# Sample attention of a decoder step: narrow products ordered by a priority of their own, the last-arriving input first, and the first head's key parts split off one step ahead

## The chip, the cores and the metric

The kernel runs on one core of one Trainium2 chip. The metric is the device time of one execution in microseconds. A core has five engines with queues of their own: TensorE (PE: matrix products; PEld is its weight load, which overlaps), VectorE (DVE), ScalarE (ACT), GpSimd (POOL) and SyncE (SP). Each engine takes the instructions of its queue strictly in order. An instruction whose input isn't there holds back everything behind it on that engine.

## The reference, cut to what matters

One layer of a hybrid decoder: a gated FFN, token mixing (differential attention beside an mLSTM), and a second gated FFN. It is computed for a prompt of 512 tokens, and for 8 samples with 4 new tokens each, whose attention looks back on 512 tokens in a paged cache. The change touches the attention: that of the samples, and the first block of that of the prompt.

```
past_k = cache_k[l][page_table].reshape(DB, -1, H_ATT, ATT_KDIM)
past_v = cache_v[l][page_table].reshape(DB, -1, H_ATT, ATT_DV)
...
logits = jnp.einsum('bqhcd,bkhcd->bchqk', q, k) * (ATT_DQ ** -0.5)
logits = jnp.where(mask, logits + bias, -jnp.inf)
p = jax.nn.softmax(logits, axis=-1)
a = p[:, 0] - lam * p[:, 1]
return jnp.einsum('bhqk,bkhd->bqhd', a, v)
```

All arrays are float32. There are 4 heads with keys of 2 x 64 and values of 128 columns, and 4 cache pages of 128 tokens for each sample.

## The kernel before, in words

**Wide products.** The activations lie transposed, channels on the partitions, in two halves of 288 and 256 tokens. Each weight tile of 128x128 is split into a high and a low part (L210 on ACT, L211 on DVE), and `mm3` issues three products for each tile: L224, L225, L226. A half of one output tile takes 8 tiles of 128 channels, so 24 such products of 288 or 256 columns stand in a row.

**Side work.** While the projections of the mixing stage run (`run(project(...))` in `mix`), every half of a projection is followed by one step of a set of generators: `attn_head` (queue "prep"), `attn_block` (queue "attn"), `attn_samples` (queue "smp"), and the mLSTM's. A step traces a few instructions, up to its `yield`. The order of the instructions on each engine is then made at compile time by a scheduler: of the instructions that it holds to be ready it takes the one of the highest priority, and the priority follows the order in which the program traced them. `high_priority(offset=...)` raises it for what is traced in its block; `issue_after(ins)` puts what its block traces on an engine behind `ins` there.

**Prompt attention.** `key_parts` splits a head's keys into high and low parts (L936 on ACT, L937 on DVE), `query_parts` does it for the 128 queries of a block (L946, L948; their tile `vb` exists once). The products of queries and keys are L964. In the kernel before, the first step of `attn_block` for block 0 of a head makes the parts, and its second step issues L964.

**Sample attention.** `attn_samples` works through two groups g of four samples j. Pages come by an indirect DMA that POOL issues (`page`, L1013) into the tile `pgin`, of which there are 7. Key pages are transposed (L1039), copied by ACT (L1040) to `pgT` (3 of it), and multiplied with the queries in *narrow* products: L1027 has only 32 columns of weights, one for each head, in four column strips of the array (`tile_position=(0, 32 * h)`). One call of `scores` makes 4 of them, and two calls come together. L1066 does the same for the new keys. After the softmax (L1069 to L1092), narrow products of 512 columns follow: four with the new values (L1098), and for each of the 4 value pages pg four with the cached values (L1102), one for each sample j. The four value pages for pg + 1 are requested after the four products of pg are traced. At that point three of the seven `pgin` tiles hold key pages ahead for g = 1, while g = 0 runs, and four hold the value pages in use. A narrow product of one strip can run beside those of the other three. In fp32 each of them is two instructions in the trace.

The queue of POOL holds, besides the page requests, the loads and stores of the mLSTM's states (L1212, L1279) and small copies (L1459).

Of the kernel before, what the change touches and what calls it, by code (L numbers as in the profile page):

```python
# [22 lines left out]
NS = NB * NT  # L23
# [6 lines left out]
NPG = PAST // PAGE  # L30
H = 4
# [22 lines left out]
AHEAD = 3  # L54
NBK = 32
# [123 lines left out]
class _Builder:  # L179
# [722 lines left out]
    def attn_head(self, h, k, v, side):  # L902
        nc = self.nc
        hd = self.hd
        kt = hd.tile([128, 4, 128], F32, name="kt")
        vt = hd.tile([128, 4, 132], F32, name="vt")
        for qb in range(4):
            side.add("attn", self.attn_block(h, qb, self.X[:, 4 + h, :], k, vt))
            if qb < 2:
                yield  # L910
# [40 lines left out]
    def attn_block(self, h, qb, q, k, vt):  # L951
        nc = self.nc
        wk = self.wk
        n = (qb + 1) * 128
        if qb == 0:
            self.key_parts(k)
            self.query_parts(q[:, 0:n])
            yield
# [35 lines left out]
        po = self.ps_tile()  # L994
# [11 lines left out]
    def attn_samples(self):  # L1006
# [14 lines left out]
        for g in range(2):  # L1021
# [3 lines left out]
            def scores(p, j, kT):  # L1025
                for h in range(H):
                    nc.tensor.matmul(lg[32 * h:32 * h + 32, p * 256:p * 256 + 256], lhsT=self.qz[:, 4 * g + j, h, :],  # L1027
                                     rhs=kT[:, h, :], start=j == 0, stop=j == 3, tile_position=(0, 32 * h))
            for p in range(NPG // 2):
                for j in range(4):  # L1030
# [10 lines left out]
                    if len(todo_scores) == 2:  # L1041
                        while todo_scores:
                            scores(*todo_scores.pop(0))
# [18 lines left out]
            while todo_scores:  # L1062
                scores(*todo_scores.pop(0))
            for j in range(4):
                for h in range(H):
                    nc.tensor.matmul(ln[32 * h:32 * h + 32, 0:NS], lhsT=self.qz[:, 4 * g + j, h, :], rhs=self.kas[:, h, :],  # L1066
                                     start=j == 0, stop=j == 3, tile_position=(0, 32 * h))
# [28 lines left out]
            for j in range(4):  # L1096
                sj = slice(32 * j, 32 * j + 32)
                nc.tensor.matmul(po[sj, :], lhsT=an[:, sj], rhs=vtok, start=True, stop=False, tile_position=(0, 32 * j))  # L1098
            for pg in range(NPG):
                for j in range(4):  # L1100
                    sj = slice(32 * j, 32 * j + 32)
                    nc.tensor.matmul(po[sj, :], lhsT=aT[:, pg * 128 + 32 * j:pg * 128 + 32 * j + 32], rhs=vps[j],  # L1102
                                     start=False, stop=pg == NPG - 1, tile_position=(0, 32 * j))
# [544 lines left out]
```

## Time and profile before

| what | value |
|---|---|
| time, median of 3 runs | 1174.2 us (1172.94 to 1174.42) |
| time of the profiled execution | 1173.48 us |
| span of the profiled execution | 1171.7 us |
| PE, PEld busy | 1156.8 us, 1119.6 us |
| DVE, ACT, POOL busy | 655.0 us, 524.5 us, 114.4 us |
| mean granted TensorE clock | 0.996 |

The span runs from the first instruction to the last, and the execution's own time has 1.8 us around it. In this kernel TensorE is busy nearly always, so the useful views are those that show where it is not: the stretches (busy time and granted clock in windows), what it waited for, and the order of time. Matmuls are pipelined, so the start of one to the start of the next tells what it costs; the duration of a single one in the profile is longer.

### The profile page before, as it was taken

To read this page: it belongs to the slowest core of one execution; us is meant where nothing else is said; L and a number is where in the kernel's file an instruction comes from. 1 tells how busy PE (TensorE), PEld (TensorE's weight loads), DVE (VectorE), ACT (ScalarE), POOL (GpSimd) and SP (SyncE) were. 2 spreads that over 40 slices of the span, in tenths; PEclk is the share of its full clock that TensorE was granted. 3 is DMA by queue.
4 is the path that set the end of the run, shared out by engine and by line. 5 is a ranking of instruction groups with operands and counts; after the bars stand their busy time and mean duration, and the time that the engine had idled before them with its cause. 6 is when DMAs were issued, how large, how long until landed. Compare 5 with 4: busy or idle time off the path is not lost. (4 is left out here: it accounts for less than half of the span.)

```text
span 1171.7 us, 22966 instructions
## 1 busy us (share of the span) xinstructions
PE 1156.8 (99%) x9202; PEld 1119.6 (96%) x9202; DVE 655.0 (56%) x1633; ACT 524.5 (45%) x1259; POOL 114.4 (10%) x155
## 2 busy tenths in 40 slices
PE   8999999999999999999999999999999999999997
PEld 8999999999999999899789879999999999999997
DVE  6655454544223698668676567885555454522334
ACT  6533332333323565667555566763333332332333
POOL 0000000000000043421234441000000000000000
PEclk9999999999999999999999999999999999999999
DMA  7322322232333464543355644532322323133333
GB/s 190 127 73 76 105 91 90 73 98 75 100 95 104 137 178 142 174 133 86 98 158 165 197 148 156 168 106 75 109 73 74 108 85 97 50 100 99 100 100 126
DMA packets 157545, 132.89 MB, mean 113 GB/s; under 512 B 5437, under 2 KB 149157, under 8 KB 157440
## 3 DMA queue, kind: packets, MB, share of 16 engines
q1 hardware_dynamic: 146576, 102.00, 29.8%
q0 software_dynamic: 8624, 27.05, 7.3%
q10 hardware_dynamic: 2240, 2.38, 0.7%
q8 instruction: 72, 1.18, 0.4%
q14 instruction: 33, 0.27, 0.1%
HBM read 122.35 MB, written 9.59 MB: 113 GB/s over the span
## 5 line engine op out<-in xcount | busy, mean ns | idle before, releaser
L224 PE MATMUL acc<-h,wh 128*128 128x256 f32 (+1 forms) x1896 | 552.6, 292 | 0.0
L225 PE MATMUL acc<-h,wh 128*128 128x256 f32 (+1 forms) x1896 | 547.6, 289 | 0.0
L226 PE MATMUL acc<-h,wl 128*128 128x256 f32 (+1 forms) x1896 | 545.0, 287 | 0.0
L211 DVE TENSOR_TENSOR wl<-raw,wh 128x512 fp32r<-128x512 f32 x378 | 251.2, 675 | 206.4 <-ACT wh L210 203.1
L224 PEld LDWEIGHTS acc<-h,wh 128*128 128x128 f32 x1896 | 357.0, 188 | 8.2 <-issue 7.5
L226 PEld LDWEIGHTS acc<-h,wl 128*128 128x128 f32 x1896 | 358.0, 189 | 0.7 <-issue 0.6
L225 PEld LDWEIGHTS acc<-h,wh 128*128 128x128 f32 x1896 | 357.3, 188 | 0.9 <-issue 0.4
L210 ACT CAST wh<-raw 128x512 fp32r<-128x512 f32 x378 | 225.6, 607 | 254.1 <-PE acc L225 208.9
L225 PE MATMUL acc<-ul,wh 128*128 128x288 f32 (+1 forms) x704 | 202.6, 288 | 0.0
L224 PE MATMUL acc<-uh,wh 128*128 128x288 f32 (+1 forms) x704 | 202.3, 287 | 0.0
L226 PE MATMUL acc<-uh,wl 128*128 128x288 f32 (+1 forms) x704 | 201.8, 287 | 0.0
L224 PEld LDWEIGHTS acc<-uh,wh 128*128 128x128 f32 x704 | 132.2, 188 | 0.1
L225 PEld LDWEIGHTS acc<-ul,wh 128*128 128x128 f32 x704 | 132.2, 188 | 0.1
L226 PEld LDWEIGHTS acc<-uh,wl 128*128 128x128 f32 x704 | 132.2, 188 | 0.1
L413 ACT CAST uh<-uu 128x288 fp32r<-128x288 f32 x88 | 36.9, 419 | 148.1 <-DVE uu L412 148.1
L411 DVE TENSOR_TENSOR uu<-acc,r 128x288 f32<-128x288 f32 (+1 forms) x84 | 37.0, 440 | 112.1 <-PE acc L226 106.8
L404 ACT ACTIVATE sg<-sg 128x288 f32<-128x288 f32 (+1 forms) x84 | 35.9, 430 | 93.6 <-DVE sg L396 93.6
L396 DVE TENSOR_TENSOR sg<-acc,r 128x288 f32<-128x288 f32 x84 | 37.0, 441 | 56.9 <-PE acc L226 52.4
L414 DVE TENSOR_TENSOR ul<-uu,uh 128x288 fp32r<-128x288 f32 x88 | 38.6, 439 | 22.1 <-ACT uh L413 22.0
L412 DVE TENSOR_TENSOR uu<-uu,sg 128x288 f32<-128x288 f32 x88 | 38.8, 441 | 7.1 <-ACT sg L404 1.6
L1335 POOL DMA_DIRECT2D x_keep<-X x2 | 1.8, 896 | 359.8 <-DVE X L327 359.8
L1013 POOL DMA_INDIRECT pgin<-in_cache_v_dram,idx x32 | 33.2, 1037 | 34.9 <-PE smp L1039 15.3
(388 smaller groups left out, 1088.2 us busy)
## 6 DMA issues: line engine op xcount, KB each, us to landing
raw<-in_ffn_w_gate_dram SPq DMA_DIRECT2D x20, 1024.0 KB, 5.3
raw<-in_ffn_w_up_dram SPq DMA_DIRECT2D x20, 1024.0 KB, 5.3
raw<-in_ffn_w_down_dram SPq DMA_DIRECT2D x20, 1024.0 KB, 6.1
raw<-in_w_in_dram SPq DMA_DIRECT2D x28, 512.0 KB, 4.6
raw<-in_ffn_w_down_dram SPq DMA_DIRECT2D x20, 384.0 KB, 3.6
raw<-in_w_out_dram SPq DMA_DIRECT2D x7, 1024.0 KB, 5.9
raw<-in_ffn_w_gate_dram SPq DMA_DIRECT2D x4, 512.0 KB, 5.9
raw<-in_ffn_w_up_dram SPq DMA_DIRECT2D x4, 512.0 KB, 6.9
```

What stands on the lines that cost most here:

```text
L210: nc.scalar.copy(out=wh[:, 0:n], in_=s)
L211: nc.vector.tensor_tensor(out=wl[:, 0:n], in0=s, in1=wh[:, 0:n].bitcast(F32), op=ALU.subtract)
L224: nc.tensor.matmul(ps, lhsT=wh, rhs=xh(k0 + k), start=st, stop=False)
L225: nc.tensor.matmul(ps, lhsT=wh, rhs=xl(k0 + k), start=False, stop=False)
L226: self.last_mm = nc.tensor.matmul(ps, lhsT=wl, rhs=xh(k0 + k), start=False, stop=sp).ins
L396: nc.vector.tensor_tensor(out=sg, in0=pg, in1=self.rs(hs, half), op=ALU.mult)
L404: nc.scalar.activation(out=sg, in_=sg, func=AF.Silu)
L411: nc.vector.tensor_tensor(out=uu, in0=pu, in1=self.rs(hs, half), op=ALU.mult)
L412: nc.vector.tensor_tensor(out=uu, in0=uu, in1=sg, op=ALU.mult)
L413: nc.scalar.copy(out=uh[:, m, sl], in_=uu)
L414: nc.vector.tensor_tensor(out=ul[m][:, sl], in0=uu, in1=uh[:, m, sl].bitcast(F32), op=ALU.subtract)
L1013: nc.gpsimd.indirect_dma_start(out=t[:, 0:512], out_offset=None, in_=caches[which], in_offset=IndirectOffsetOnAxis(ap=self.idx[:, b * NPG ...
```

## The change

Three edits, in `attn_samples`, `attn_head` and `attn_block`.

First, the narrow products get a priority far above their place in the program (`AHEAD_OF`), each group of 8 or 4 in a block of its own. Second, their order is turned: the newest key tile first in `scores`, the newest head first in the products with the new keys, the last-requested page first with the values. The products with the new keys come before the last scores (`issue_after`). Third, `attn_head` makes the key and query parts of head 0 itself, yields, and only then adds the blocks; block 0 of head 0 then yields without making them.

```diff
+AHEAD_OF = 20000
...
         kt = hd.tile([128, 4, 128], F32, name="kt")
         vt = hd.tile([128, 4, 132], F32, name="vt")
+        if h == 0:
+            self.key_parts(k)
+            self.query_parts(self.X[:, 4, 0:128])
+            yield
         for qb in range(4):
...
         if qb == 0:
-            self.key_parts(k)
-            self.query_parts(q[:, 0:n])
+            if h:
+                self.key_parts(k)
+                self.query_parts(q[:, 0:n])
             yield
...
-            def scores(p, j, kT):
-                for h in range(H):
-                    nc.tensor.matmul(lg[32 * h:32 * h + 32, p * 256:p * 256 + 256], lhsT=self.qz[:, 4 * g + j, h, :],
-                                     rhs=kT[:, h, :], start=j == 0, stop=j == 3, tile_position=(0, 32 * h))
+            def scores(todo):
+
+                with self.tc.high_priority(offset=AHEAD_OF):
+                    for p, j, kT in reversed(todo):
+                        for h in range(H):
+                            nc.tensor.matmul(lg[32 * h:32 * h + 32, p * 256:p * 256 + 256],
+                                             lhsT=self.qz[:, 4 * g + j, h, :], rhs=kT[:, h, :],
+                                             start=j == 1, stop=j == 2, tile_position=(0, 32 * h))
+                todo.clear()
...
                     if len(todo_scores) == 2:
-                        while todo_scores:
-                            scores(*todo_scores.pop(0))
+                        scores(todo_scores)
...
-            while todo_scores:
-                scores(*todo_scores.pop(0))
-            for j in range(4):
-                for h in range(H):
-                    nc.tensor.matmul(ln[32 * h:32 * h + 32, 0:NS], lhsT=self.qz[:, 4 * g + j, h, :], rhs=self.kas[:, h, :],
-                                     start=j == 0, stop=j == 3, tile_position=(0, 32 * h))
+            with self.tc.high_priority(offset=AHEAD_OF):
+                for j in range(4):
+                    for h in reversed(range(H)):
+                        mm = nc.tensor.matmul(ln[32 * h:32 * h + 32, 0:NS], lhsT=self.qz[:, 4 * g + j, h, :],
+                                              rhs=self.kas[:, h, :], start=j == 0, stop=j == 3, tile_position=(0, 32 * h))
+            with self.tc.issue_after(mm.ins):
+                scores(todo_scores)
...
             po = self.smp.tile([128, 512], F32, name="smp")
-            for j in range(4):
-                sj = slice(32 * j, 32 * j + 32)
-                nc.tensor.matmul(po[sj, :], lhsT=an[:, sj], rhs=vtok, start=True, stop=False, tile_position=(0, 32 * j))
-            for pg in range(NPG):
+            with self.tc.high_priority(offset=AHEAD_OF):
                 for j in range(4):
                     sj = slice(32 * j, 32 * j + 32)
-                    nc.tensor.matmul(po[sj, :], lhsT=aT[:, pg * 128 + 32 * j:pg * 128 + 32 * j + 32], rhs=vps[j],
-                                     start=False, stop=pg == NPG - 1, tile_position=(0, 32 * j))
+                    nc.tensor.matmul(po[sj, :], lhsT=an[:, sj], rhs=vtok, start=True, stop=False, tile_position=(0, 32 * j))
+            for pg in range(NPG):
+                with self.tc.high_priority(offset=AHEAD_OF):
+                    for j in (3, 2, 1, 0):
+                        sj = slice(32 * j, 32 * j + 32)
+                        nc.tensor.matmul(po[sj, :], lhsT=aT[:, pg * 128 + 32 * j:pg * 128 + 32 * j + 32], rhs=vps[j],
+                                         start=False, stop=pg == NPG - 1, tile_position=(0, 32 * j))
                 if pg < NPG - 1:
                     vps = [page(1, 4 * g + j, pg + 1) for j in range(4)]
```

The scheduler makes another order from it. Lines of the changed kernel have other numbers: L1116 there is L1102 here, L1111 is L1098, L1037 is L1027, L971 is L964, L1051 is L1039, and L226 to L228 are the wide products. What a row waits for is named by its semaphore: DMASW for a DMA issued by POOL, one of eight in turn.

**TensorE, the value products of the second page, first group of samples, before** (L964 is another head's attention, L1176 the mLSTM):

```order
L964 MATMUL aux<-cs,vb 128x384 [waits Activation_49]
L964 MATMUL aux<-cs,vb 128x384 [waits DVE_49]
L1102 MATMUL smp<-pgin,saT 32x512 [waits DMASW4_49]
L1176 MATMUL aux<-vt,kt 128x130 [waits DVE_49]
L1102 MATMUL smp<-pgin,saT 32x512 [waits DMASW5_49]
L1102 MATMUL smp<-pgin,saT 32x512 [waits DMASW6_49]
L1102 MATMUL smp<-pgin,saT 32x512 [waits DMASW7_49]
L224 MATMUL acc<-h_4527,wh 128x288
```

One of the four stands apart from the other three, with an mLSTM product between them.

**TensorE, from the first page's products to the second's, same group, now** (L997 and L893 are transposes and products of other side work, L1169 the mLSTM's, L900 a transpose; the rows left out are the rest of one half of a projection, 24 wide products in all):

```order
L1116 MATMUL smp<-pgin,saT 32x512 [waits DMASW5_49]
L1116 MATMUL smp<-pgin,saT 32x512 [waits DMASW4_49]
L997 MATMUL aux<-base,L 128x128 x3
L1169 MATMUL aux<-rw,sel_5155 128x512 [waits DVE_49]
L893 MATMUL aux<-base,v 128x128 [waits DVE_49]
L893 MATMUL aux<-base,v 128x128 x3
L226 MATMUL acc<-h_4527,wh 128x288
...
L900 MATMUL aux<-base,y 128x128 [waits Activation_49]
L1116 MATMUL smp<-pgin,saT 32x512 [waits DMASW7_49]
L1116 MATMUL smp<-pgin,saT 32x512 [waits DMASW6_49]
L1116 MATMUL smp<-pgin,saT 32x512 [waits DMASW5_49]
L1116 MATMUL smp<-pgin,saT 32x512 [waits DMASW4_49]
```

The four stand together, the last-requested page first. From the end of one page's four to the next page's four stood 65, 59 and 67 other products in group 0 before, for the first, second and third gap, and now 33, 29 and 29. In group 1 it was 34, 30 and 31 and is now 15, 20 and 17.

**TensorE, the first block of head 0, before** (L964 on the parts of head 0; the rows around it are two halves of projections):

```order
L226 MATMUL acc<-h_4834,wl 128x256
L964 MATMUL aux<-cs,vb 128x128 x4
L224 MATMUL acc<-h_4527,wh 128x288
```

and now:

```order
L228 MATMUL acc<-h_4834,wl 128x256
L226 MATMUL acc<-h_4527,wh 128x288
...
L228 MATMUL acc<-h_4527,wl 128x288
L971 MATMUL aux<-cs,vb 128x128 x4
L1051 MATMUL smp<-base,pgin 128x128 x8
```

The half of 24 products of 288 columns that followed the four now stands ahead of them. POOL's queue keeps the order of the value page requests in group 0; in group 1 some requests move past state stores and a small copy.

## The prediction

> **What bounds the kernel now.** I read the page's first part, then the stretches, then the order of time where TensorE has gaps.
>
> ```profile
> PE 1156.8 (99%) x9202; PEld 1119.6 (96%) x9202; DVE 655.0 (56%) x1633; ACT 524.5 (45%) x1259; POOL 114.4 (10%) x155
> 110.00:330.00 220.00, 220.00 (x1759) 220.00 (x1758) 101.25 (x195) 72.68 (x143) 0.00 (x0) 1.00 0.28 85
> ```
>
> TensorE is busy 99% of the span, and the next engine 56%. So TensorE sets the end: an edit gains what it takes off TensorE's queue in start-to-start time, and loses what TensorE then waits. The second row is a stretch of wide products alone (the columns after the time are PE, PEld, DVE, ACT, POOL, then the granted clock, 1.00). It gives 220/1759 = 0.125 us for one product of 272 columns on average, thus 0.132 at 288 and 0.118 at 256.
>
> What else stands in the mixing stage is priced from the order of time, start to start:
>
> ```profile
> 506.81 0.60 PE L891 MATMUL aux<-base,k 128*128 128x128 f32 x4
> 507.25 1.06 PE L996 MATMUL aux<-vt,aT 128*128 128x128 f32 x8
> 508.14 0.49 PE L990 MATMUL aux<-base,L 128*128 128x128 f32 x3
> 508.47 0.60 PE L1039 MATMUL smp<-base,pgin 128*128 128x128 f32 x4
> ```
>
> Four transposes cost 0.44 us, four plain fp32 products (8 instructions) 0.89, three transposes 0.33.
>
> **Term 1: narrow products that stand together.** A whole group of scores, a split one, a split group of values and a whole one:
>
> ```profile
> 489.32 1.07 PE L1027 MATMUL smp<-pgT,qz 128*32 128x256 f32 x16
> 490.32 0.39 PE L224 MATMUL acc<-h,wh 128*128 128x256 f32 x1
> ...
> 501.73 1.05 PE L1027 MATMUL smp<-pgT,qz 128*32 128x256 f32 x10
> 502.71 0.66 PE L1039 MATMUL smp<-base,pgin 128*128 128x128 f32 x4
> 503.29 0.63 PE L1027 MATMUL smp<-pgT,qz 128*32 128x256 f32 x6
> 503.86 0.39 PE L224 MATMUL acc<-h,wh 128*128 128x256 f32 x1
> ...
> 578.89 1.05 PE L1102 MATMUL smp<-pgin,saT 128*32 128x512 f32 x2
> 579.87 0.49 PE L1176 MATMUL aux<-vt,kt 128*128 128x130 f32 x2
> 580.29 1.06 PE L1102 MATMUL smp<-pgin,saT 128*32 128x512 f32 x6
> 581.27 0.40 PE L224 MATMUL acc<-h,wh 128*128 128x288 f32 x1
> ...
> 602.11 1.07 PE L1102 MATMUL smp<-pgin,saT 128*32 128x512 f32 x8
> 603.11 0.40 PE L224 MATMUL acc<-h,wh 128*128 128x288 f32 x1
> ```
>
> A whole score group takes 490.32 - 489.32 = 1.00 us; the split one 0.98 + 0.57 = 1.55. One value product alone takes as long as all four: 0.98 + 0.98 = 1.96 split, 1.00 whole. The order before has four score groups split (5 and 3 of 8) and four value groups (1 and 3 of 4); the changed one has none. That is 4 x 0.55 + 4 x 0.96 = **-6.0 us**. The groups now often stand behind a wide product rather than a transpose, in the middle of a half. Entering and leaving so is not cleanly shown before, nor is how long a score group at the head of the queue waits for ACT's copy. I bound this by the split's own surplus: 12 such groups at 0 to 0.25 us (under half of 0.55), so 0 to +3, less the small waits on other engines that happen to vanish, down to -3. I take 0, since the two have the same size.
>
> **Term 2: the first block of head 0.**
>
> ```profile
> 459.00:461.00 2.00, 0.80 (x4) 1.00 0.70 236
> 461.00:463.00 2.00, 1.82 (x9) 0.71 0.49 148
> 463.00:465.00 2.00, 2.00 (x10) 0.50 1.00 247
> 465.00:467.00 2.00, 2.00 (x17) 0.93 1.09 359
> ```
>
> Here the columns are PE's busy time and the granted clock. TensorE idles 1.20 + 0.18 = 1.38 us at L964, and then the clock falls to half for a while: 2 x (0.29 + 0.50 + 0.07) = 1.72 us lost. Together 3.1. What the change puts ahead of L964:
>
> ```profile
> 457.51 1.26 ACT L936 CAST cs<-k 64x512 fp32r<-64x512 f32 x2
> 458.50 1.40 DVE L937 TENSOR_TENSOR cs<-k,cs 64x512 fp32r<-64x512 f32 x2
> 458.80 1.26 ACT L946 CAST vb<-X 64x128 fp32r<-64x128 f32 x4
> 459.47 0.33 PE L964 MATMUL aux<-cs,vb 128*128 128x128 f32 x1 [0.44 <-ACT vb L946]
> 459.92 1.20 DVE L948 TENSOR_TENSOR vb<-X,vb 64x128 fp32r<-64x128 f32 x4
> ```
>
> L964 stood ready from 459.47 - 0.44 = 459.03; behind 24 products of 288 columns (3.2 us) it comes at 462.2. The last part is made at 459.92 + 1.20 = 461.1, and up to there ACT and DVE keep their order. So the parts are hidden by that half with 1.1 us to spare, the clock has no reason to fall, and the term is **-3.1 us**. Without the cover it is 0. The step costs no instruction, and no DMA is issued or passed in it.
>
> **Term 3: the value pages come no sooner.** This term speaks against the change. A group's four products free four `pgin` tiles, POOL requests the next four pages into them, and the next group needs all four. In the first gap of group 0:
>
> ```profile
> 568.03 1.04 PE L1102 MATMUL smp<-pgin,saT 128*32 128x512 f32 x8
> 569.00 0.40 PE L224 MATMUL acc<-h,wh 128*128 128x288 f32 x1
> ...
> 569.33 1.03 POOL L1013 DMA_INDIRECT pgin<-in_cache_v_dram,idx  x1 [0.75 <-PE smp L1102]
> 570.66 0.98 POOL L1013 DMA_INDIRECT pgin<-in_cache_v_dram,idx  x1 [0.30 <-issue]
> 571.96 0.95 POOL L1013 DMA_INDIRECT pgin<-in_cache_v_dram,idx  x1 [0.30 <-issue]
> 573.21 0.95 POOL L1013 DMA_INDIRECT pgin<-in_cache_v_dram,idx  x1 [0.31 <-PE aux L964]
> ...
> pgin<-in_cache_v_dram,idx POOLq DMA_INDIRECT x32, 3.6
> ```
>
> POOL waits for L1102, requests a page every 1.3 us, and a request lands 3.6 us after its issue (median of 32, last row). So from the end of one group (569.00) to the last page of the next: 573.21 + 3.6 - 569.00 = 7.8 us. Before, the next group began at 578.89, 9.9 us after: hidden. By the changed order TensorE has much less in between:
>
> - gap 1: 3 transposes 0.33, L1169 about 0.3 (taken as another three), 4 transposes 0.44, 24 x 0.132 = 3.2, one transpose 0.1: 4.4 us
> - gap 2: 8 plain products 1.8, 21 x 0.118 = 2.5: 4.3 us
> - gap 3: 3 x 0.118 + 15 x 0.132 = 2.3, 8 products of L964 about 1.4, 3 others 0.6: 4.3 us
>
> The narrow priority outranks all other ready work, so the next group stands at the head of the queue and TensorE waits: 3.4 + 3.5 + 3.5 = **+10.4 us**. Turning the order of the four helps nothing here: the last page is awaited whole, and behind it wait the wide products, thus everything. Bounds: with landing at 3.3 and at 5.2 (least and greatest of a stretch below) it is 9.5 to 15.
>
> In group 1 no key pages are ahead any more, so three of the four pages are requested a group sooner. Gap 1 has 10 x 0.118 + 0.3 + 0.44 = 1.9 us of work, and needs one page: 0.3 + 3.6 = 3.9, a wait of 2.0. Gap 2 has about 2.7 (12 instructions of mLSTM products, 4 transposes, 6 wide). Its last page is fifth in POOL's row after the first group: 4 x 1.3 + 0.3 + 3.6 = 9.1, while TensorE arrives at 3.9 + 1.0 + 2.7 = 7.6, a wait of 1.5. Gap 3 has 17 x 0.132 = 2.3; its last page can be asked for once group 2 is through (10.1), lands at 10.1 + 0.3 + 3.6 = 14.0, against 12.4: 1.6. Sum 5.1. The order before waited for a page too:
>
> ```profile
> 701.63 1.05 PE L1102 MATMUL smp<-pgin,saT 128*32 128x512 f32 x4
> 703.01 1.05 PE L1102 MATMUL smp<-pgin,saT 128*32 128x512 f32 x2 [0.33 <-DMA pgin<-in_cache_v_dram,idx]
> ...
> DMA to landing us min/median/max: 3.3/3.7/5.2
> ```
>
> Those six instructions took 703.01 - 701.63 = 1.38 for the first four and so about 0.9 us of wait, since a whole group of eight takes 1.00. That goes. Group 1: **+4.2 us**, with bounds 2 and 7.
>
> **Term 4: the clock.** Term 2 shows 1.38 us of idle TensorE followed by 3.4 us at half clock, 1.7 us lost. Within the six gaps a slow clock costs nothing, because TensorE only arrives later at the same page. After the last gap of a group it does: 1.7 for group 0, and half of that for group 1, where a wait of 1.6 may fall across two stretches: **+2.5 us**, bounds 0 and 3.4. The Trainium skill (page "TensorE: Matmul & The Clock Gate", section "Part 1: The HAM clock gate (the "warmup" mystery)") has the clock fall to half after an idle window of about 3.4 us. By that rule waits of 1.6 us would leave the clock alone and those of 3.5 us only now and then lower it, and the sum would be 2.5 lower. The trace disagrees: there the clock fell after 1.38 us.
>
> **Sum.** -6.0 - 3.1 + 10.4 + 4.2 + 2.5 + 0 = +8.0 us on the profiled execution's 1173.5 (span 1171.7 and 1.8 around it): 1181.5. The median of the runs shown is 0.7 above that execution, so 1182. Some of term 3 should be given back: while TensorE waits, ACT and DVE run ahead, and L964's own waits within the gaps (the parts of a block at 461 above cost tenths) fall into time already lost. I take 1 us for it and forecast **1181 us**.
>
> **The rivals.**
>
> *The pages are there in time (faster).* If the requests were spread, or TensorE's work between two groups were longer than counted, terms 3 and 4 fall away, and even the old wait of 0.9 goes: 1174.2 - 6.0 - 3.1 - 0.9 = 1164. For it speaks only that the changed order was made by a scheduler that held the pages to be ready there. Against it speak the rows of POOL: 7.8 us against 4.4, and no row in which a page lands within 3.3 us. It decides from a landing under 0.5 us. Chance 0.10.
>
> *The gains and the waits cancel.* If the gaps cost half, say because other products in them wait for ACT and DVE so that TensorE arrives 1.5 us later, term 3 is about 8 and term 4 one: 1174.2 - 9.1 + 8 + 1 = 1174. For it: gap 3 of group 0 holds eight L964, each behind its parts. Against: gaps 1 and 2 hold none. Chance 0.22.
>
> *Every gap ends cold (slower still).* If POOL's requests fall behind other DMAs on its queue (two loads and a store of states stand among the requests of group 1), or if each gap's half clock delays the release of the next pages as well, six times 1.7 is paid instead of 2.5, and landing goes to 5.2 in some: 1181 + 8 = 1189. The Trainium skill's section "HAM oscillation — how this bites in real kernels" on the same page describes this pattern, work between two transfers that is shorter than the transfer. Chance 0.13.
>
> *The edit does not do what it says.* The order shows all 16 groups whole, so splitting can only return as a wait within a group, for which the last-first order leaves little: below 0.05, and within the ranges.
>
> **How the numbers follow.** The forecast's own case has 0.55, with a range of 1176.5 to 1186. A measurement of this kernel can tell about 0.2%, 2.3 us, from no change: faster is below 1171.9, slower above 1176.5. Faster: the first rival 0.10 and a fifth of the second, 0.14. Within: three fifths of the second and a little of the forecast's low end, 0.17. Slower: 0.69. The range that holds 8 in 10 leaves out the first rival and the far end of the third: 1171 to 1188.
>
> **What would show each step.** Term 1: L1116 and L1037 (L1102 and L1027 here) stand in the order of time only as x8 and x16, about 1.0 us each. Term 2: no idle TensorE at 459 to 467, and clock 1.00 there. Term 3: the list of waits has the value products behind the DMA of `pgin` with some 10 us and more, in six places, and the first group's gaps are 7 to 9 us long from group to group. Term 4: clock below 1.00 in the stretches that hold the value products. The forecast is wrong if the value products wait less than 6 us in sum, or if term 2's stall only moves to the transposes that now follow L964, or to the products of the next block.

## The result, and the profile after

The changed kernel takes **1189.6 us** (median of 4 runs, 1187.7 to 1190.6) against 1174.2 for the kernel before: a ratio of **1.0129** (95% interval 1.0117 to 1.0142), 15 us slower. The forecast was 1181 with a range up to 1188: the direction was right, and the change forecast, 7 us, was under half of what came. The profiled execution has a span of 1188.0 us. Of the page of the changed kernel, the busy times:

```profile
PE 1157.9 (97%) x9202; PEld 1122.4 (94%) x9202; DVE 656.5 (55%) x1633; ACT 523.3 (44%) x1259; POOL 113.4 (10%) x155
```

Of its list of waits (us in total, times, longest):

```profile
PE smp L1116 <- DMA pgin<-in_cache_v_dram,idx: 13.7, 6, 4.3
PE acc L227 <- DVE h L1494: 1.7, 1, 1.7
PE aux L971 <- ACT vb L952: 1.4, 3, 1.0
PE acc L226 <- ACT y L311: 0.8, 1, 0.8
```

TensorE's busy time is 1.1 us more than before and the span 16.3 us longer: TensorE waits, and the largest wait is the one that the prediction named, for value pages, in six places. In the order of time the eight groups of value products read:

```profile
565.74 1.04 PE L1116 MATMUL smp<-pgin,saT 128*32 128x512 f32 x8
574.56 1.94 PE L1116 MATMUL smp<-pgin,saT 128*32 128x512 f32 x8 [3.32 <-DMA pgin<-in_cache_v_dram,idx]
584.17 1.07 PE L1116 MATMUL smp<-pgin,saT 128*32 128x512 f32 x8 [1.23 <-DMA pgin<-in_cache_v_dram,idx]
594.22 1.93 PE L1116 MATMUL smp<-pgin,saT 128*32 128x512 f32 x8 [4.33 <-DMA pgin<-in_cache_v_dram,idx]
...
689.37 1.04 PE L1116 MATMUL smp<-pgin,saT 128*32 128x512 f32 x8
694.00 1.06 PE L1116 MATMUL smp<-pgin,saT 128*32 128x512 f32 x8 [1.55 <-DMA pgin<-in_cache_v_dram,idx]
700.47 1.93 PE L1116 MATMUL smp<-pgin,saT 128*32 128x512 f32 x8 [2.75 <-DMA pgin<-in_cache_v_dram,idx]
705.94 1.06 PE L1116 MATMUL smp<-pgin,saT 128*32 128x512 f32 x8 [0.57 <-DMA pgin<-in_cache_v_dram,idx]
```

All groups are whole, and three of them take 1.93 instead of 1.05: they ran at half clock. The stretches of half clock around them (the clock is the third column from the end):

```profile
573.80:580.60 6.80, 6.04 (x27) 4.38 (x28) 0.41 (x2) 1.35 (x5) 2.93 (x4) 0.50 0.26 70
594.30:597.70 3.40, 3.40 (x15) 1.74 (x16) 0.00 (x0) 0.00 (x0) 1.01 (x2) 0.50 0.00 0
700.10:703.50 3.40, 3.03 (x13) 1.37 (x14) 0.00 (x0) 0.00 (x0) 1.41 (x2) 0.50 0.45 160
```

POOL's last request after the first group, and its first and last after the second, in the order of time:

```profile
570.95 0.95 POOL L1020 DMA_INDIRECT pgin<-in_cache_v_dram,idx  x1 [0.30 <-issue]
576.75 0.95 POOL L1020 DMA_INDIRECT pgin<-in_cache_v_dram,idx  x1 [4.85 <-PE smp L1116]
...
580.52 0.95 POOL L1020 DMA_INDIRECT pgin<-in_cache_v_dram,idx  x1 [0.30 <-PE aux L1179]
```

The last request at 570.95 and 3.6 us of landing give 574.55: the second group starts at 574.56. Half the time that TensorE is busy in these stretches is lost: (6.04 + 3.40 + 3.03) / 2 = 6.2 us. With 13.7 of waits that is 19.9 us around the value products. It is not this execution alone: all four executions of the change have a mean granted clock of 0.990 to 0.992, those of the kernel before 0.994 to 0.997.

Head 0 in the changed kernel, in the order of time, where the prediction expected no wait:

```profile
463.76 0.56 PE L971 MATMUL aux<-cs,vb 128*128 128x128 f32 x4
464.41 0.30 ACT L952 CAST vb<-X 64x128 fp32r<-64x128 f32 x1 [1.31 <-PE aux L971]
...
465.52 0.40 ACT L982 ACTIVATE L<-L,z 128x128 f32<-128x128 f32 x1 [0.81 <-DVE z L981]
...
466.03 0.30 ACT L952 CAST vb<-X 64x128 fp32r<-64x128 f32 x1
...
466.38 0.50 PE L971 MATMUL aux<-cs,vb 128*128 128x256 f32 x2 [1.04 <-ACT vb L952]
...
467.54 0.39 PE L971 MATMUL aux<-cs,vb 128*128 128x256 f32 x1 [0.20 <-ACT vb L952]
```

The first block runs without a wait. The second is held up twice by ACT. ACT may write the second block's query parts into the one `vb` buffer only when TensorE has read the first block's (1.31 us). Then it stands 0.81 us for DVE's sums of the first block (L982, ahead in its queue), and writes the part that TensorE waits for at 466.03. That makes 1.04 + 0.20 = 1.24 us of idle TensorE in place of 1.38.

### The profile page after: what moved, and what is told of

Same layout as the page of the kernel before. It is cut to its first block, busy times and chain, and to the rows that moved or that the text cites. A ratio compares the mean times of both kernels' runs of the same rounds, so it can differ in the third digit from the quotient of the medians.

```text
span 1188.0 us, 22959 instructions
## 1 busy us (share of the span) xinstructions
PE 1157.9 (97%) x9202; PEld 1122.4 (94%) x9202; DVE 656.5 (55%) x1633; ACT 523.3 (44%) x1259; POOL 113.4 (10%) x155
## 4 chain that ended last, share of the span: by engine, by line
PE 90%; ACT 3%; DMA 3%; DVE 3%; issue 1%; POOL 0%; SPq 0%; DVEq 0%; ACTq 0%; POOLq 0%
PE acc L226 26%; PE acc L227 26%; PE acc L228 26%; DMA pgin<-in_cache_v_dram,idx 2%; PE smp L1051 1%; PE aux L1003 1%; PE smp L1116 1%; ACT wh L212 1%; PE aux L971 1%; PE smp L1037 1%; DMA raw<-in_ffn_w_gate_dram 1%; PE smp L226 1%; PE smp L227 1%; PE smp L228 1%; ACT vb L952 1%
## 5 line engine op out<-in xcount | busy, mean ns | idle before, releaser
L226 PE MATMUL acc<-h,wh 128*128 128x256 f32 (+1 forms) x1896 | 554.4, 293 | 0.8 <-ACT y L311 0.8
L228 PE MATMUL acc<-h,wl 128*128 128x256 f32 (+1 forms) x1896 | 546.4, 288 | 0.0
L226 PEld LDWEIGHTS acc<-h,wh 128*128 128x128 f32 x1896 | 357.8, 189 | 7.4 <-issue 5.8
L228 PEld LDWEIGHTS acc<-h,wl 128*128 128x128 f32 x1896 | 358.8, 189 | 3.3 <-issue 3.3
L226 PE MATMUL acc<-uh,wh 128*128 128x288 f32 (+1 forms) x704 | 202.5, 288 | 0.0
L228 PE MATMUL acc<-uh,wl 128*128 128x288 f32 (+1 forms) x704 | 202.0, 287 | 0.0
L226 PEld LDWEIGHTS acc<-uh,wh 128*128 128x128 f32 x704 | 132.4, 188 | 0.1
L228 PEld LDWEIGHTS acc<-uh,wl 128*128 128x128 f32 x704 | 132.3, 188 | 0.1
L1020 POOL DMA_INDIRECT pgin<-in_cache_k_dram,idx x32 | 34.2, 1069 | 35.0 <-PE smp L1051 19.2
```

The source lines that it names most:

```text
L226: nc.tensor.matmul(ps, lhsT=wh, rhs=xh(k0 + k), start=st, stop=False)
L228: self.last_mm = nc.tensor.matmul(ps, lhsT=wl, rhs=xh(k0 + k), start=False, stop=sp).ins
L1020: nc.gpsimd.indirect_dma_start(out=t[:, 0:512], out_offset=None, in_=caches[which], in_offset=IndirectOffsetOnAxis(ap=self.idx[:, b * NPG ...
```

## The experiments

All ratios are against the kernel before on the same chip, with 95% intervals. In us they are taken of 1174.

| kernel | scores | values | head 0 | ratio |
|---|---|---|---|---|
| the change | new | priority, last first | new | 1.0129 (1.0117 to 1.0142) |
| v_off | new | as before | new | 1.0015 (1.0006 to 1.0024) |
| v_lastfirst | new | last first only | new | 0.9981 (0.9972 to 0.9990) |
| v_only | as before | priority, last first | as before | 1.0125 (1.0109 to 1.0142) |
| h0_only | as before | as before | new | 1.0029 (1.0017 to 1.0041) |
| vl_no_h0 | new | last first only | as before | 0.9972 (0.9960 to 0.9984) |
| s_only | new | as before | as before | 0.9963 (0.9950 to 0.9977) |
| after_no_h0 | new | priority, last first | as before | 1.0099 (1.0086 to 1.0112) |
| after_forward | new | priority, order 0 to 3 | new | 1.0135 (1.0120 to 1.0149) |

The other eight kernels stand with their experiments. The theory was that the loss is TensorE waiting for pages that the priority makes it want too soon.

### The value products: put back, or last page first without a priority

v_off puts the value products back; v_lastfirst differs from v_off in one line. Both diffs:

```
-            with self.tc.high_priority(offset=AHEAD_OF):
...
-                    for j in (3, 2, 1, 0):
+                for j in range(4):
```

```
-                for j in range(4):
+                for j in (3, 2, 1, 0):
```

> The changed kernel with only the value products put back as they were (no priority, products in the order 0 to 3); the scores' priority and the early key parts of head 0 stay. Theory A (the loss lies in TensorE waiting for value pages that the priority made it want too soon): the six waits of L1116 on the DMA of pgin shrink to about 1 us in all, the clock is 1.00 from 560 to 720 us, and the time is 1189.6 less 13.6 to 17 of waits and slow clock plus 3.9 for the value groups that are split again: 1172 to 1177 less what varies at the start, so about 1173, just under the kernel before. Rival B (the loss lies with the scores' priority or the moved stall of head 0): the time stays above 1182. Rival C (half and half): about 1180.

> As v_off, but the four value products of a page group stand with the last-arriving page first, without a priority. In the order the groups are then whole, as in the changed kernel, and 48 wide products stand between two groups, as in the kernel before. Theory A (what costs is that a group stands too early, not that it is whole): no waits of more than about 1 us in all, and the split groups' 3.9 us are kept: 1167 to 1171, faster than the kernel before by some 0.4%. Rival D (a whole group releases four tiles at once, and the row of four requests then lands too late wherever the group stands): waits of 3 us in most gaps and about 1180 or more.

v_off came to 1175.4 us and v_lastfirst to 1171.7. The stretch from 560 to 720 us (the first number after the stretch's length is TensorE's busy time), v_off first:

```profile
560.00:720.00 160.00, 158.42 (x1279) 134.61 (x1279) 107.22 (x372) 90.18 (x278) 58.05 (x73) 1.00 0.48 151
```

And v_lastfirst:

```profile
560.00:720.00 160.00, 157.25 (x1321) 138.96 (x1319) 111.42 (x384) 93.77 (x288) 58.90 (x74) 1.00 0.50 156
```

The one row on value pages in v_lastfirst's list of waits:

```profile
PE smp L1114 <- DMA pgin<-in_cache_v_dram,idx: 1.0, 1, 1.0
```

No slow clock, and waits of 1 us at most: theory A holds against B, C and D. In v_lastfirst 48 wide products stand between two whole groups of group 0, and the pages are there. So whole groups cost nothing; their place does. Whole instead of split gained 1.0015 - 0.9981 = 0.0034, 4.0 us. That is not the prediction's 3.8, though: v_off's order breaks the value groups in six places (2, 2 and 4 instructions in one of them) where the kernel before has four, and by the same price six are 5.8, of which v_lastfirst gives back its wait of 1.0. The two further breaks are also worth the 2 us that v_off was above what was expected of it.

### Each part alone

Each of these is the kernel before with some hunks of the change's diff: v_only with the last (from `po = self.smp.tile` on), h0_only with the first (`attn_head` and `attn_block`), s_only with those between.

> The kernel before with only the value products changed (priority and last-arriving first). Theory A: the whole loss is here. 1174.2 plus waits of 14 to 17 with the clock, less 3.9 for whole value groups: 1184 to 1188. The waits stand in six places behind the DMA of pgin, and there are fewer score groups whole than in the changed kernel. Rival B (the loss needs the other parts): 1174 to 1178.

> The kernel before with only the key parts and first query parts of head 0 made a step sooner. By the prediction's second term TensorE no longer idles 1.4 us at 459 to 467 us and the clock stays at 1.00 there: 3.1 us less, 1171. By what the changed kernel's trace shows (idle time of 1.2 us moved to 465 to 469 us, at the second block's parts and the transposes behind them, but no slow clock), about 1.7 to 2 us less: 1172.3. Rival: the stall comes back whole with the next block, slow clock included: 1174.

> The kernel before with only the score products changed (grouped, with priority, products with the new keys ahead of the last scores). By the first term of the prediction four split score groups are worth 4 x 0.55 = 2.2 us: 1172. Rival, from the changed kernel's trace, where the time from 470 to 560 us fell by only about 0.5 us against the kernel before: what the whole groups save goes into waits of the transposes and of the group at the head of the queue for ACT's copy of pgT, and the time is 1173.5 to 1174.5.

v_only: 1187.9, with waits of 14.2 us in six places; the loss needs no other part. s_only: 1169.9, 4.3 us faster than before, twice the expected 2.2 (the interval, 2.7 to 5.9, leaves 2.2 out). h0_only: 1177.9, which **none of the three theories had: 3.4 us slower**. The order of h0_only shows one thing that goes with it: one more break in the score groups and two more in the value groups than before (0.55 + 2 x 0.96 = 2.5 us by term 1's prices), and one in the new values' four products of group 0. v_off has the last three of these breaks as well.

s_only leaves the value groups split in four places. Against it, vl_no_h0 (below) has them whole, and gains nothing: 0.9972 for 0.9963, within the intervals, with 4.3 us of waits for value pages in place of 0.5. vl_two_steps has waits of 0.8 there and 0.9967. So what whole value groups bring without a priority is seen in one pair of kernels only.

### Pages sooner, and no pages

k_late requests the first key pages of group 1 only behind group 0's last value pages, so that three tiles are free for value pages:

```
-                        if i < len(todo):
+                        if i < len(todo) and todo[i][0] == g:
...
                     vps = [page(1, 4 * g + j, pg + 1) for j in range(4)]
+                if g == 0 and pg == NPG - 2:
+                    ahead = [page(0, 4 * gg + jj, q) for gg, q, jj in todo[16:16 + AHEAD]]
```

> The changed kernel, with the first three key pages of group 1 requested only after the last value pages of group 0, so that three tiles of pgin are free and three of the next four value pages can be requested a group sooner. The order answers with group 0's groups closer still: 2.0, 2.2 and 1.8 us of work in its three gaps (4.3 before). Theory A (the wait is the landing of pages that can be requested only when tiles come free): the last page lands 3.9, 5.2 and 4.9 us after the end of the group ahead, so the waits are about 1.9, 2.0 and 2.1 (6.0 in all; the changed kernel's were 8.9 and two groups at half clock), and the time is 3 to 5 us below 1189.6: 1185 to 1187. Rival (the waits come from the transfers' traffic or the row of requests, not from tiles): waits of 3 to 4 us as before, 1189.

It took 1183.8 us (ratio 1.0079, 1.0065 to 1.0093), 5.9 less than the change. Its group 0, in the order of time:

```profile
570.48 1.06 PE L1116 MATMUL smp<-pgin,saT 128*32 128x512 f32 x8 [2.14 <-DMA pgin<-in_cache_v_dram,idx]
575.60 1.06 PE L1116 MATMUL smp<-pgin,saT 128*32 128x512 f32 x8 [1.59 <-DMA pgin<-in_cache_v_dram,idx]
580.49 1.07 PE L1116 MATMUL smp<-pgin,saT 128*32 128x512 f32 x8 [1.42 <-DMA pgin<-in_cache_v_dram,idx]
```

Waits of 5.2 us for 6.0 expected, and no group at half clock in this execution, the fastest of five (their mean granted clocks are 0.992 to 0.997). The rival (traffic, or the row of requests) would have left them at 3 to 4 each.

no_more_pages leaves out the requests of the next four pages:

```
-                if pg < NPG - 1:
-                    vps = [page(1, 4 * g + j, pg + 1) for j in range(4)]
```

> The changed kernel without the value pages behind the first of each group: the products of pages 1 to 3 read the tiles of page 0 again, so 24 of the 32 page loads are left out and nothing has to land between two value groups; all the products are made. The order then puts all 16 of a group in one row. Theory A (waits for pages and the slow clock behind them are the loss): 1189.6 less 8.9 and 4.9 of waits, 2 groups at half clock (0.9 each) and 1 to 2 more of slow clock behind a wait: 1171 to 1173, near v_lastfirst's 1171.7. Rival (whole groups ahead of everything cost time even when their pages are there, since the other work is pushed back behind them): 1178 or more.

Its chip ran the kernel before at 1177.3; the ratio is 0.9967 (0.9955 to 0.9979), 1170.1 of 1174. Without pages to wait for, the priority costs nothing.

after_forward only turns the four products round again, under the same priority:

```
-                    for j in (3, 2, 1, 0):
+                    for j in range(4):
```

> The changed kernel with the value products in the order 0 to 3 again, with their priority. In the order most groups then fall apart into 2, 1 and 1, with 5 to 13 wide products between, for each product is put where its own page is thought to be there: some 11 places more at about 0.96 us. Theory A: the waits come from pages, so single products wait less (the row of requests keeps moving, a tile is asked for again as soon as its product is through): waits of 5 to 8 us instead of 13.8, no half clock, and about 10 more for the splits: 1189 to 1193. Rival (the order of the four sets the loss): 1180 or less.

Ratio 1.0135, no better than the change. Its waits for pages fell to 2.5 us in all. Its value groups are broken in 11 places (10.6 us by term 1's price), and another wait is longer; two rows of its list of waits:

```profile
PE aux L971 <- ACT vb L952: 2.6, 3, 2.2
PE smp L1116 <- DMA pgin<-in_cache_v_dram,idx: 2.5, 2, 1.8
```

Under the priority the order of the four brings nothing that can be told (the intervals overlap); without it, v_lastfirst against v_off, it brought 4.0 us.

### Head 0

after_no_h0 is the change without its first hunk, the one of `attn_head` and `attn_block`.

> The changed kernel without the earlier key parts of head 0. The prediction's second term took them for a gain of 3.1 us: 1192.5 without them. By the pairs h0_only and the kernel before (+3.9), and v_off and s_only (+5.5), they cost: 1184 to 1186. Third theory: they cost only where they split value groups (h0_only and v_off, but not here, where all are whole): 1188 to 1190.

Ratio 1.0099: 3.5 us less than the change, as the pairs said, and not more, as the prediction said. The third theory (it costs only where it splits value groups) falls, since here none is split.

vl_no_h0 is v_lastfirst without the early parts; vl_h0_buffer is v_lastfirst with a buffer of their own for the first block's query parts:

```
-            self.query_parts(self.X[:, 4, 0:128])
+            self.query_parts(self.X[:, 4, 0:128], self.pg.tile([128, H, 256], F32R, name="pgT", bufs=3)[:, :, 0:128])
```

> As v_lastfirst (scores' priority, value products last-arriving first without a priority), without the earlier key parts of head 0. In both orders all narrow groups are whole, so this shows what the early key parts cost or bring by themselves. Theory E (they bring a little: the 1.4 us stall at 459 us with its 1.7 us of slow clock against a stall of 1.3 us at 465 us and a wait of 0.9 us near 740 us that is seen only with them): about 1 us slower than v_lastfirst, 1172.5. Rival F (h0_only's loss of 3.9 us is of the early parts themselves and not of the order around them): 2 to 4 us faster than v_lastfirst, 1168 to 1169.5.

> As v_lastfirst, with the first query parts of head 0 in a buffer of their own (a pgT buffer, free there) in place of the single vb buffer. Theory W (the moved stall is ACT's write of the second block's query parts into vb, which must wait until TensorE has read the first block's): ACT L952's wait on L971 near 464 us goes, and TensorE's idle time at 463 to 469 us falls from about 1.4 us to under 0.4; 1.0 to 1.5 us faster than v_lastfirst, 1170.4. Rival (the chain of ACT and DVE steps behind the parts is late by itself): the idle time stays above 1 us and the time as v_lastfirst's.

vl_no_h0: ratio 0.9972, 1 us below v_lastfirst within overlapping intervals; neither theory. The groups are not alike in the two: in v_lastfirst one of the four products with the new values of group 0 stands apart. vl_h0_buffer: 0.9999 (0.9990 to 1.0008), 2 us slower than v_lastfirst, where 1.3 less was expected. The wait of ACT is gone and another took its place, in the order of time:

```profile
463.57 0.45 PE L973 MATMUL aux<-cs,vb 128*128 128x256 f32 x2
...
465.86 0.28 DVE L981 CUSTOM_DVE_ANT_0 L<-aux,strip 128x128 f32<-128x128 f32 x1
...
466.30 0.47 PE L973 MATMUL aux<-cs,vb 128*128 128x256 f32 x2 [2.28 <-DVE z L981]
```

The stretch behind it:

```profile
467.00:469.00 2.00, 2.00 (x11) 2.00 (x10) 1.49 (x9) 1.90 (x8) 0.00 (x0) 0.50 1.08 337
```

The second block now comes at once, and TensorE then stands until DVE has read the first block's result (its read starts at 465.86); the half clock (0.50) follows. So the two blocks stand too close; a buffer doesn't help. Not all of the 2 us need come from here: the wait for a value page is 2.4 us in this kernel and 1.0 in v_lastfirst.

What else the edit of head 0 does, its order tells: the order of every engine is word for word that of a kernel in which head 0 has the extra step alone, and its key parts stay where they were. **The edit is a shift of all later side work by one step.** The last experiments stand on vl_two_steps: vl_no_h0 with a second step between two value groups of group 1:

```
-                if g == 0:
-                    yield
+                yield
                 yield
```

> As vl_no_h0 (scores' priority, value products last-arriving first without a priority, no early key parts), with two steps of the other work between two value groups of group 1 too, as group 0 has them; 48 wide products then stand in two of its three gaps instead of 24. Theory A (what costs is the distance between a group and the next against the landing of its pages): the one wait of 3.5 us at 695 us and the slow clock behind it go, all value groups stay whole, 1166 to 1168, faster than both kernels. Rival (the sample work now ends later, and what waits for it at the end of the stage pays): 1170 to 1172.

> vl_two_steps again, as the ground for the next three on the same chip: 0.997 of the kernel before (its ratio was 0.9967).

Both times the ratio was 0.9967 (together 0.9954 to 0.9979). The wait of 3.5 us of vl_no_h0 is gone, but against vl_no_h0's 0.9972 the ratio shows no difference; 1166 to 1168 wasn't reached, and 1170 is the rival's figure. Then the edit of head 0 (two_h0), the same with one step fewer between head 0's second and third block (two_h0_back), and with two steps between its first and second (two_h0_apart). In the last two only the step stands ahead, which gives the same order. Of their diffs against vl_two_steps, two_h0_back:

```
+        for _ in range(1 if h == 0 else 0):
+            yield
         for qb in range(4):
...
-            if qb < 2:
+            for _ in range(((1, 0, 0, 0) if h == 0 else (1, 1, 0, 0))[qb]):
                 yield
```

and in two_h0_apart the first tuple is `(2, 1, 0, 0)`.

> vl_two_steps with the change's edit of head 0. The order of every engine is word for word the same if only the extra step is put in and the key parts stay where they were, so the edit is nothing but a shift of all later side work by one step. All narrow groups but one (new keys of group 0, 1 and 3) stay whole. Theory S (the local gain of 1 to 2 us is outweighed by what the shift moves into a worse place later): 1 to 3 us slower than two_again, 0.998 to 1.000. The prediction's second term: 3.1 us faster, 0.994.

> As two_h0, but head 0 gives the step back after its second block (one step less there), so that the order of TensorE is the same as in two_again from some 40 us later on. Theory S: only the local gain is left, the wait of 0.8 us near 740 us that every kernel with the edit shows is gone, and it is 0 to 2 us faster than two_again, 0.995 to 0.997. Rival P (the edit costs at head 0 itself, by the stall of the second block and what comes behind it): as two_h0 or slower.

> vl_two_steps with head 0's first block one step later and its second another step later, so that 32 and 37 products stand between its first three blocks. If the stall is the one buffer of query parts, used again too soon, TensorE has no idle time over 0.3 us between 452 and 485 us and the clock stays at 1.00 there: locally 1.4 us and now and then 1.7 of slow clock are gained. Theory S: the shift of two steps costs 1 to 3 later all the same, so 0.996 to 0.999. Rival (the stall is inherent in head 0's chain of parts, exponentials and sums): idle time of 1 us or more between 452 and 500 us.

| kernel | ratio |
|---|---|
| two_again | 0.9967 (0.9957 to 0.9977) |
| two_h0 | 0.9979 (0.9971 to 0.9988) |
| two_h0_back | 0.9951 (0.9938 to 0.9964) |
| two_h0_apart | 0.9948 (0.9935 to 0.9961) |

In two_h0_back the second block of heads 1 and 3 comes ahead of their first and so takes the parts of the head before; the work is the same. The stretch from 460 to 468 us in two_again:

```profile
460.00:468.00 8.00, 6.78 (x33) 6.03 (x34) 7.45 (x32) 6.25 (x20) 4.46 (x5) 0.79 0.79 243
```

In two_h0:

```profile
460.00:468.00 8.00, 6.71 (x53) 6.31 (x52) 7.12 (x30) 5.75 (x17) 3.99 (x5) 1.00 0.90 266
```

Three rows of two_h0's list of waits:

```profile
PE aux L1271 <- DMA cs<-in_state_C_dram: 2.9, 1, 2.9
PE smp L1051 <- ACT pgT L1052: 1.5, 3, 0.6
...
PE acc L226 <- ACT y L311: 0.8, 1, 0.8
```

The stretch in two_h0_back:

```profile
460.00:468.00 8.00, 6.60 (x52) 6.20 (x51) 7.20 (x24) 6.07 (x19) 4.61 (x6) 1.00 0.81 237
```

And in two_h0_apart:

```profile
460.00:468.00 8.00, 8.00 (x65) 7.74 (x64) 7.08 (x24) 5.66 (x18) 5.21 (x6) 1.00 0.72 215
```

The stretch behind the wait for the state load, in two_h0 and then in two_h0_back:

```profile
710.00:715.00 5.00, 4.84 (x31) 3.56 (x32) 3.98 (x9) 0.45 (x1) 0.00 (x0) 0.66 0.45 145
710.00:715.00 5.00, 5.00 (x40) 5.00 (x39) 3.48 (x8) 3.66 (x8) 0.00 (x0) 1.00 0.96 308
```

two_h0 has more products through in the same 8 us (53 to 33, in part since the clock stayed up) and is not faster: 1.4 us slower by the ratios, within their intervals. Its waits for a state load (2.9 us, against 1.0 in two_again) and for L311 (0.8, not in two_again) come later, and behind the state load the clock falls: 5 x 0.34 = 1.7 us lost from 710 to 715 us, none in two_again. With the step given back it is 3.3 us faster (0.9979 - 0.9951; the intervals don't meet), though the second block's stall is still there (8.00 - 6.60 = 1.40 us idle): the rival that had the cost at head 0 itself falls. Between 700 and 745 us of the two profiles, 2.9 - 1.8 = 1.1 us of the state load's wait, the 1.7 of slow clock and the 0.8 for L311 are gone, less a wait of 0.8 for a value page; elsewhere two_h0_back waits 1.8 us for a key page, which two_h0 does not.

two_h0_apart has no idle TensorE from 460 to 468 and the lowest ratio of all, **6.1 us below the kernel before**, with two_h0_back within its interval. Theory S had it at 0.996 to 0.999. It has the later costs of two_h0 too (2.7 us for the state load, a clock of 0.68 from 705 to 710 us, 0.8 for L311), but it comes to them sooner: the 4009th wide product starts at 608.6 us in it and at 611.7 in two_h0, and the last one 3.1 us sooner, too. Besides the stall, it is without the break in the new values of group 0 that two_h0 and two_h0_back have (the one broken group of two_h0, called new keys above). So a shift of two steps did not cost more than a shift of one: the price depends on where each later step falls.

## Why the prediction missed, by its own steps

The three parts in a row, by the ratios and as they were forecast:

| step | kernels | measured | forecast |
|---|---|---|---|
| scores (term 1) | before to s_only | -4.3 | -2.2 |
| values (terms 1, 3, 4, give-back) | s_only to after_no_h0 | +16.0 | -3.8 + 14.6 + 2.5 - 1 = +12.3 |
| head 0 (term 2) | after_no_h0 to the change | +3.5 | -3.1 |

**Term 2 failed**, by 6.6 us and in its sign. The rest missed by 1.6 together, but only because two misses cancel: the scores gained 2.1 more than forecast, and the values lost 3.7 more. Term 2's words were that "the parts are hidden by that half" and "The step costs no instruction". Both are true, and the first block waits for nothing. But the stall went to the second block, which the prediction had only among the things that would make it wrong, and it left out that an added step moves every later step of the side work. The idle time hardly fell (1.24 us for 1.38). The slow clock at head 0 did go in these profiles, and over all their executions two_h0 has a mean granted clock of 0.996 and two_again 0.994, about 2 us; still two_h0 is no faster, and the change is slower than after_no_h0. That the shift carries a cost is shown on two_h0, where giving the step back brought 3.3 us (with two blocks turned round in heads 1 and 3, too). Which later waits make up the 3.5 us in the change itself is not settled. Some go with the shift: the 0.8 us for L311 is there in the change, v_off and two_h0, and not in s_only, two_again or two_h0_back; the wait of the transposes of key pages for ACT's copy (L1051 on L1052) is 1.5 us in the change, v_off and two_h0, 0.6 in after_no_h0, s_only and two_again, and 0.8 in two_h0_back. The state load's wait is 1.0 in two_again, 1.8 with the step given back, 2.9 and 2.7 in two_h0 and two_h0_apart; the change has none.

**Term 3 was right** in its mechanism and its sum. From group to group 8.8 us were forecast (7.8 and the group's 1.0): the changed kernel has 8.8, 9.6 and 10.05 in group 0. In group 1 it waits 1.55 + 2.75 + 0.57 = 4.9 for 5.1 forecast; that these agree is partly luck, since 2.0, 1.5 and 1.6 were forecast for the single gaps. k_late moved the waits of group 0 as its arithmetic said, and no_more_pages took them away.

**Term 4 was mis-sized**: 2.5 forecast, 6.2 lost. The step that failed reads "Within the six gaps a slow clock costs nothing, because TensorE only arrives later at the same page". The page is not the same: a group at half clock frees its tiles 0.9 us later, so POOL asked at 576.75 and the time from group to group grew from 8.8 to 9.6. The third of these times, 10.05, is long by its last page. POOL's first and last request in it:

```profile
585.49 0.95 POOL L1020 DMA_INDIRECT pgin<-in_cache_v_dram,idx  x1 [4.01 <-PE smp L1116]
...
589.26 1.02 POOL L1020 DMA_INDIRECT pgin<-in_cache_v_dram,idx  x1 [0.31 <-PE aux L971]
```

The requests come at the usual distance, but from the last one to TensorE's start at 594.22 it is 4.96 us, where 3.6 was taken. Why this page took longer isn't settled. In part the two terms pay for each other, since TensorE at half clock comes later and waits less (1.23 instead of 3.5): both together were 18.0 forecast and 19.9 measured.

**Term 1** for the values is borne out in part: 4.0 us for six breaks in v_off and v_lastfirst, where 0.96 each would be 5.8, and no gain from s_only to vl_no_h0, where new waits for pages stand against it. For the scores it was half of what came; why whole score groups bring 4.3 instead of 2.2 isn't settled. It isn't the clock: the executions of s_only and those of the kernel before on its chip both have 0.996 in the mean.

The rival "every gap ends cold" gave 1189 for the sum, in part for its reason: a group at half clock did delay the release of the next pages (by 0.9 us), and one awaited page took 4.96 us. But three groups of six ended cold, not all, and its sum counts term 2 as a gain, so that the number itself is luck.

## What to carry to other kernels

A group of products that must wait for a transfer gains nothing from standing early: putting the last-arriving operand first kept it whole, which brought 4.0 us in one pair of kernels, and a priority on top moved it in front of its pages and cost 15 to 17 us (after_no_h0 against vl_no_h0, the change against v_lastfirst). An edit that adds a step to one of several interleaved streams shifts all that follows; compare it with the step added alone, and with the step given back further on. The price of a stall is its own length plus what the clock does behind it, and that second part is not the same in every execution.

## What the runs showed of the hardware

The half clock comes in stretches of 3.4 us or twice that (3.40 and 6.80 above), and the idle time that brings it does not decide alone. The kernel before idles 1.38 us at head 0 and s_only 1.45, for the same parts, and only the former fell to half clock. The stretch of 3.41 us ahead of the half clock in the kernel before, at 461.85:

```profile
458.44:461.85 3.41, 2.03 (x14) 1.55 (x13) 3.24 (x9) 3.29 (x9) 2.80 (x3) 1.00 0.62 169
```

In s_only the idle time falls into two such stretches:

```profile
459.65:463.06 3.41, 2.72 (x22) 2.37 (x20) 2.80 (x6) 3.13 (x8) 2.53 (x3) 1.00 0.67 190
463.06:466.47 3.41, 2.65 (x15) 2.05 (x16) 3.26 (x15) 3.20 (x11) 2.50 (x4) 1.00 0.67 188
```

In h0_only about 1.5 us of idle time brought it; in after_forward 2.2 did not, spread as in s_only. h0_only's stretches:

```profile
465.00:467.00 2.00, 0.70 (x6) 0.50 (x5) 1.54 (x10) 1.10 (x5) 1.46 (x3) 1.00 0.99 305
467.00:469.00 2.00, 1.82 (x14) 1.61 (x14) 1.60 (x9) 1.93 (x7) 0.00 (x0) 0.91 1.00 293
469.00:471.00 2.00, 2.00 (x11) 2.00 (x11) 1.56 (x9) 1.90 (x8) 0.00 (x0) 0.50 0.88 275
```

And after_forward's:

```profile
463.00:465.00 2.00, 1.32 (x12) 1.12 (x11) 1.22 (x3) 0.00 (x0) 1.70 (x2) 1.00 0.69 194
465.00:467.00 2.00, 0.44 (x3) 0.44 (x4) 1.39 (x9) 1.55 (x6) 0.72 (x2) 1.00 1.15 321
...
469.00:471.00 2.00, 2.00 (x19) 1.94 (x17) 1.55 (x9) 1.90 (x8) 0.25 (x2) 1.00 0.36 117
```

That would follow if the clock were set by windows of 3.4 us that run by themselves, and a stall counted by how much of one window it fills. The starts of the three stretches of half clock in the change speak for it: they lie 20.5 and 105.8 us apart, 6 and 31 times 3.41 or 3.42. Laid out so, in steps of 3.413 us from a stretch of half clock in each of the 18 profiles (30 to 1150 us, windows at full clock), 13 windows hold 1.9 us or more of idle TensorE, and half clock followed all of them; it followed 6 of the 41 with 1.0 to 1.9, and none of the 4614 with less. What decides between 1.0 and 1.9 stays open. The Trainium skill (page "TensorE: Matmul & The Clock Gate", section "Part 1: The HAM clock gate (the "warmup" mystery)") speaks of such a free-running window. The lengths agree with it; that a whole idle window is needed does not, since about 1.5 us were enough. So one execution of a kernel says little about a stall of 1 to 2 us: the same stall may cost 1.7 us more or not. Kernels that differ by so little have to be compared over several executions.
